# 1/rms spread over the partitions: from diagonal matrices to broadcast columns

## The chip, the core and the metric

The kernel runs on one core of a Trainium2 chip. The metric is the device time of one execution in microseconds (us). Before the change it is 2209.36 us, the median of three runs (2209.26 to 2209.65).

## The reference

One decoder layer over a sequence of 2048 tokens with 1024 features, all in float32. It normalizes x, projects it to the inputs of two groups of heads (a gated linear recurrence "HGRN" with four heads, and a sliding-window attention with eight heads), mixes their outputs back, and then runs a gated MLP of width 2816 with a short causal convolution. RMS norms stand at four places; three of them go over the 1024 features of a token, and one over the 128 values of an HGRN head.

```python
def rmsnorm(x, w, eps=EPS):
    xf = x.astype(jnp.float32)
    inv = lax.rsqrt(jnp.mean(xf * xf, axis=-1, keepdims=True) + eps)
    return (xf * inv * w.astype(jnp.float32)).astype(x.dtype)
...
    for l in range(DEPTH):
        u = rmsnorm(h, norm_mix_w[l])
        proj = u @ w_in[l]
...
        o_hg = rmsnorm(o_hg, hg_norm_w[l]).reshape(B, S, HG_VAL_WIDTH)
...
        h = h + mix @ w_out[l]
        v = rmsnorm(h, norm_ffn_w[l])
        gate = causal_depthwise_conv(v @ w_gate[l], conv_w[l], conv_b[l])
        h = h + (jax.nn.silu(gate) * (v @ w_up[l])) @ w_down[l]
    return rmsnorm(h, final_norm_w)
```

## The kernel before

The sequence is processed in two halves of 1024 tokens. Everything is held transposed: features on the 128 partitions, tokens along the free dimension. A matrix of float32 values is split into two float32r parts, high and low, and a product is made of three passes (high x high, low x high, high x low), so that the large products are streams of matmuls with 512 moving columns (`unit`, L190; `pair_unit`, L731; `product`, L915).

For each half the stages are: load and split of x, the projections and the heads (`hgrn` and `attend`, which are interleaved as generators), the output projection (`out_proj`), the gate and up projections (`gate_up`), and the down projection (`down`), which also loads the x of the next half or, in the second half, writes the output (`finish`). The gate, up and down products use a scheme with seven instead of eight block products, whose operands are sums formed on VectorE, and whose results accumulate in the banks X, Y and Z; ScalarE must copy X out between two of its products (L747).

The weight of a norm is folded into the operands; 1/rms of a token is applied to the results. It is a value per token, so it lies along the free dimension and has to be the same on all 128 partitions. This is the work of the class `Stats`:

- `add` squares one tile of features and adds it into `acc`, a tile of 128 partitions by the tokens.
- `inverse` sums `acc` over the partitions: for each 128 tokens, one matmul with that piece of `acc` as weights and one column of ones moving (L249). The sums come out with the tokens on the partitions, one column for each 128 tokens. `rsqrt` turns them into 1/rms with thirteen operations on VectorE (L158 to L168), an integer estimate and three Newton steps. Then one VectorE operation multiplies the unit matrix `ident` with these columns (L253), so that `acc` holds one diagonal matrix for each 128 tokens.
- `spread` multiplies a matrix of ones with these diagonal matrices, 512 columns at a time (L263): the sum over partitions of a diagonal matrix is its diagonal, now on every partition. ScalarE copies the result from its bank into `acc` (L266), or, where `bank` is given, the reader takes it from the bank.

There are nine such pairs of inverse and spread: over 1024 tokens for the first norm of each half ("x") and for the second ("h", during the first gate unit), over 512 tokens for three parts of the final norm ("o", "o2"), and over 256 tokens for the last two quarters. `rsqrt` is also called eight times in `hgrn` (L581). `ident` is made at the start by GpSimd (L84 to L87) and is also the moving operand of the transposes (L336, L408, L553, L592) and the mask of the diagonal blocks (L459).

The order of the instructions on each engine is set by a scheduler at build time: it simulates the program, and so a change at one place can change the order elsewhere. The pool `hp` with the tag "m" has eight slots, which tiles take in turn; the x tiles of the first load are its first users. 

Of the kernel before, what the change touches and what calls it, by code (L numbers as in the profile page):

```python
# [8 lines left out]
F32 = mybir.dt.float32  # L9
F32R = mybir.dt.float32r  # L10
U32 = mybir.dt.uint32
I32 = mybir.dt.int32
AF = mybir.ActivationFunctionType
ALU = mybir.AluOpType
# [3 lines left out]
P = 128  # L18
D = 1024
KT = D // P  # L20
# [10 lines left out]
EPS = 1e-6  # L31
# [18 lines left out]
def hymba_layer(ctx: ExitStack, tc: tile.TileContext, a: dict, out: bass.AP):  # L50
    nc = tc.nc

    def pool(name, bufs=1, space=None, stack=ctx, **kw):
        if space is not None:
            kw["space"] = space
        return stack.enter_context(tc.tile_pool(name=name, bufs=bufs, **kw))

    cp = pool("const")
    xp = pool("x")
    wp = pool("w")  # L60
    hp = pool("h")
    sp = pool("small", bufs=2)
# [6 lines left out]
    def ps(kind, name):  # L69
        return spaces[kind].tile([P, 512], F32, tag=kind, name=name)  # L70
# [3 lines left out]
    def halves():  # L74
# [5 lines left out]
    ones = cp.tile([P, P], F32, name="ones")  # L80
    nc.vector.memset(ones, 1.0)
    warm = cp.tile([P, 1], F32, name="warm")
    nc.scalar.activation(warm, ones[:, 0:1], AF.Sigmoid)
    ident = cp.tile([P, P], F32, name="ident")  # L84
    nc.gpsimd.memset(ident, 1.0)
    nc.gpsimd.affine_select(out=ident, in_=ident, compare_op=ALU.is_equal, fill=0.0,
                            base=0, pattern=[[-1, P]], channel_multiplier=1)  # L87

    idle = ps("at", "idle")
    for _ in range(WARM):  # L90
# [63 lines left out]

    def rsqrt(ss, n, scale, keep=None):

        ms = sp.tile([P, n], F32, tag=f"ms{n}", name="ms")
        nc.vector.tensor_scalar(ms, ss, scale, EPS, op0=ALU.mult, op1=ALU.add)  # L158
        y = sp.tile([P, n], F32, tag=f"y{n}{keep}", name="y")
        yi = y.bitcast(I32)  # L160
        nc.vector.tensor_scalar(yi, ms.bitcast(I32), 1, None, op0=ALU.logical_shift_right)
        nc.vector.tensor_scalar(yi, yi, -1.0, float(0x5F3759DF), op0=ALU.mult, op1=ALU.add)
        nc.vector.tensor_scalar(ms, ms, -0.5, None, op0=ALU.mult)
        t = sp.tile([P, n], F32, tag=f"t{n}", name="t")
        for _ in range(3):
            nc.vector.tensor_tensor(t, y, y, op=ALU.mult)
            nc.vector.tensor_tensor(t, t, ms, op=ALU.mult)
            nc.vector.scalar_tensor_tensor(y, t, 1.5, y, op0=ALU.add, op1=ALU.mult)  # L168
        return y
# [56 lines left out]
    class Stats:  # L226
# [16 lines left out]
        def inverse(self, keep):  # L243

            n = self.acc.shape[-1]
            nt = n // P
            st = ps("hg", "pst")
            for c in range(nt):
                nc.tensor.matmul(st[:, c:c + 1], self.acc[:, c * P:(c + 1) * P], ones[:, 0:1],  # L249
                                 start=True, stop=True)  # L250
            rs = self.rs = rsqrt(st[:, 0:nt], nt, 1.0 / D, keep)
            dg = self.acc
            return nc.vector.tensor_tensor(dg.rearrange("p (c t) -> p c t", t=P),  # L253
                                    ident.unsqueeze(1).to_broadcast([P, nt, P]),
                                    rs.unsqueeze(2).to_broadcast([P, nt, P]), op=ALU.mult)

        def spread(self, bank=None):

            n = self.acc.shape[-1]
            w = min(n, 512)  # L260
            for b in range(n // w):
                pb = ps(aux[b % 2 if bank is None else bank], "pinv")[:, 0:w]
                nc.tensor.matmul(pb, ones, self.acc[:, b * w:(b + 1) * w], start=True, stop=True)  # L263
                if bank is not None:
                    return pb
                nc.scalar.copy(self.acc[:, b * w:(b + 1) * w], pb)  # L266
# [166 lines left out]
    def hgrn(hf, h, X, invb, vs, WG, mix, p, fu=None):  # L433
# [140 lines left out]
        for c in range(TT):  # L574
# [4 lines left out]
            marks["po"] = nc.tensor.matmul(o, Q[:, cs], prev, start=False, stop=True)  # L579
            nc.scalar.activation(on[:, c], o, AF.Square, accum_out=ss[:, c:c + 1])  # L580
        rs = rsqrt(ss, TT, 1.0 / P)  # L581
        if h == HG - 1:
            mix[h] = new_x()
# [441 lines left out]
    for hf in range(NH):  # L1025
        X, kv, invb, rs, f0 = nxt
        with ExitStack() as st:
            p = pool(f"mix{hf}", stack=st, reuse_waits="tile")
# [36 lines left out]
        with ExitStack() as st:  # L1065
            p = pool(f"ffn{hf}", stack=st, reuse_waits="tile")
# [64 lines left out]
```

## Time and profile before

| | |
|---|---|
| median of 3 runs | 2209.36 us |
| the profiled execution, its time | 2211.5 us |
| the profiled execution, its span (first to last instruction) | 2209.8 us |
| mean granted clock of TensorE | 0.995 |
| instructions | 29508 |

In the lines of the profile, PE is TensorE (matmul), PEld its weight loads, DVE VectorE, ACT ScalarE, POOL GpSimd, SP SyncE. A line of the timeline gives the start in us, the duration in us, the engine, the line of the kernel, the operation, the tiles written and read, the shape, and how many instructions are merged; in brackets stands how long the engine was idle before, and what ended that. A duration of several merged instructions reaches from the first start to the last end. Matmuls are pipelined, so the step from one start to the next is what a matmul costs, not its duration. A line of the windows gives for a stretch the busy time of PE, PEld, DVE, ACT and POOL (with their instructions), the granted clock of TensorE, the busy share of the DMA engines, and GB/s.

### The profile page before, as it was taken

To read this page: it belongs to the slowest core of one execution; us is meant where nothing else is said; L and a number is where in the kernel's file an instruction comes from. 1 tells how busy PE (TensorE), PEld (TensorE's weight loads), DVE (VectorE), ACT (ScalarE), POOL (GpSimd) and SP (SyncE) were. 2 spreads that over 40 slices of the span, in tenths; PEclk is the share of its full clock that TensorE was granted. 3 is DMA by queue.
4 is the path that set the end of the run, shared out by engine and by line. 5 is a ranking of instruction groups with operands and counts; after the bars stand their busy time and mean duration, and the time that the engine had idled before them with its cause. 6 is when DMAs were issued, how large, how long until landed. Compare 5 with 4: busy or idle time off the path is not lost.

```text
span 2209.8 us, 29508 instructions
## 1 busy us (share of the span) xinstructions
PE 2182.2 (99%) x11406; PEld 1832.6 (83%) x11406; DVE 1643.8 (74%) x2488; ACT 1050.9 (48%) x1845; POOL 6.3 (0%) x27
## 2 busy tenths in 40 slices
PE   9999999999999999999999999999999999999998
PEld 7988988878888888888889889888788888888887
DVE  6568568688887888786856666577888888887766
ACT  6446554464444445335625455535544444444353
POOL 1000000000000000000000000000000000000000
PEclk9999999999999999999999999999999999999999
DMA  4101112323233234964631111204132323259643
GB/s 154 50 30 50 37 43 68 121 71 112 95 113 101 96 119 159 374 219 162 200 124 51 36 43 41 67 29 142 55 128 82 125 90 119 95 190 388 226 136 129
DMA packets 94214, 257.91 MB, mean 117 GB/s; under 512 B 11578, under 2 KB 17402, under 8 KB 94074
## 3 DMA queue, kind: packets, MB, share of 16 engines
q1 hardware_dynamic: 88128, 251.70, 33.6%
q10 hardware_dynamic: 5946, 4.34, 0.7%
q8 instruction: 89, 1.46, 0.3%
q14 instruction: 51, 0.42, 0.1%
HBM read 195.10 MB, written 57.15 MB: 114 GB/s over the span
## 4 chain that ended last, share of the span: by engine, by line
PE 94%; DVE 4%; ACT 1%; DMA 0%; issue 0%; SPq 0%; DVEq 0%; ACTq 0%
PE X L741 7%; PE X L743 7%; PE X L742 7%; PE pop L208 6%; PE hq L208 4%; PE q L208 4%; PE f L208 4%; PE g L208 4%; PE pdx L923 4%; PE pdx L924 4%; PE pdx L925 4%; PE Y L741 4%; PE Y L742 4%; PE Y L743 4%; PE pdy L924 3%; PE pdy L923 3%
## 5 line engine op out<-in xcount | busy, mean ns | idle before, releaser
L619 ACT CAST whi<-raw 128x1024 fp32r<-128x1024 f32 x88 | 92.7, 1053 | 104.3 <-PE X L742 64.5
L742 PE MATMUL X<-T,whi 128*128 128x512 f32 x352 | 136.9, 389 | 0.0
L743 PE MATMUL X<-T,wlo 128*128 128x512 f32 x352 | 136.9, 389 | 0.0
L741 PE MATMUL X<-T,whi 128*128 128x512 f32 x352 | 136.9, 389 | 0.0
L807 DVE SCALAR_TENSOR_TENSOR y<-ga,cw,y 128x1024 f32<-128x1024 f32 x88 | 112.5, 1278 | 30.9 <-ACT y L805 30.9
L747 ACT COPY u<-X 128x512 f32<-128x512 f32 x88 | 51.6, 586 | 130.0 <-PE X L743 129.6
L620 DVE TENSOR_TENSOR wlo<-raw,whi 128x1024 fp32r<-128x1024 f32 x88 | 107.1, 1217 | 0.0
L184 ACT CAST whi<-raw 128x1024 fp32r<-128x1024 f32 (+2 forms) x61 | 62.7, 1034 | 82.1 <-PE q L208 31.9
L620 DVE TENSOR_TENSOR xld<-raw,xhd 128x1024 fp32r<-128x1024 f32 x72 | 80.7, 1131 | 19.8 <-ACT xhd L619 19.5
L619 ACT CAST xhd<-raw 128x1024 fp32r<-128x1024 f32 x72 | 69.7, 978 | 43.8 <-DMA raw<-act0T 15.8
L208 PE MATMUL pop<-XL,whi 128*128 128x512 f32 x256 | 86.7, 396 | 2.1 <-DVE XL L220 2.1
L208 PE MATMUL pop<-XH,wlo 128*128 128x512 f32 x256 | 85.5, 392 | 0.7 <-DVE wlo L185 0.7
L208 PE MATMUL pop<-XH,whi 128*128 128x512 f32 x256 | 85.1, 398 | 0.2
L185 DVE TENSOR_TENSOR wlo<-raw,whi 128x1024 fp32r<-128x1024 f32 (+2 forms) x61 | 73.0, 1203 | 9.0 <-ACT whi L184 9.0
L741 PEld LDWEIGHTS X<-T,whi 128*128 128x128 f32 x352 | 66.1, 188 | 13.7
L742 PEld LDWEIGHTS X<-T,whi 128*128 128x128 f32 x352 | 66.1, 188 | 13.7
L743 PEld LDWEIGHTS X<-T,wlo 128*128 128x128 f32 x352 | 66.1, 188 | 13.7
L923 PE MATMUL pdx<-xhd,hid 128*128 128x512 f32 x192 | 74.3, 391 | 1.0 <-ACT hid L619 1.0
L924 PE MATMUL pdx<-xld,hid 128*128 128x512 f32 x192 | 74.8, 389 | 0.0
L741 PE MATMUL X<-T,Sh 128*128 128x512 f32 x176 | 69.0, 392 | 5.4 <-ACT s L747 5.4
L925 PE MATMUL pdx<-xhd,lod 128*128 128x512 f32 x192 | 73.7, 389 | 0.0
L611 PE MATMUL pvv<-whi,XH 128*128 128x256 f32 x256 | 73.5, 288 | 0.0
(362 smaller groups left out, 6564.9 us busy)
## 6 DMA issues: line engine op xcount, KB each, us to landing
wr<-in_w_down SPq DMA_DIRECT2D x90, 512.0 KB, 5.1
raw<-in_w_gate SPq DMA_DIRECT2D x44, 512.0 KB, 3.6
raw<-in_w_up SPq DMA_DIRECT2D x44, 512.0 KB, 3.5
raw<-act0T SPq DMA_DIRECT2D x20, 512.0 KB, 5.5
raw<-act1T SPq DMA_DIRECT2D x20, 512.0 KB, 10.1
act0B<-y SPq DMA_DIRECT2D x33, 256.0 KB, 2.5
act1B<-y SPq DMA_DIRECT2D x33, 256.0 KB, 2.3
raw<-in_w_out SPq DMA_DIRECT2D x16, 512.0 KB, 5.5
```

Of the source, the lines that this page charges most:

```text
L185: nc.vector.tensor_tensor(lo[:, c], raw[:, c], hi[:, c].bitcast(F32), op=ALU.subtract)
L208: nc.tensor.matmul(o[b], w, x[:, bs], start=f, stop=l)
L611: nc.tensor.matmul(o[:, 0:256], xh[:, t], hi[:, c], start=kt == 0, stop=False)
L619: nc.scalar.copy(h, src)
L620: (eng or nc.vector).tensor_tensor(l, src, h.bitcast(F32), op=ALU.subtract)
L741: nc.tensor.matmul(o, wh[:, ws], xh, start=i == 0 and not more, stop=False, skip_group_check=more)
L742: nc.tensor.matmul(o, wh[:, ws], xl, start=False, stop=False, skip_group_check=more)
L743: nc.tensor.matmul(o, wl[:, ws], xh, start=False, stop=i == 3, skip_group_check=more)
L807: nc.vector.scalar_tensor_tensor(y, g[:, w:w + HALF], C.cw[:, ft, w:w + 1], y, op0=ALU.mult, op1=ALU.add)
L923: nc.tensor.matmul(o, wh[:, i, c], ah[:, i, cols], start=f, stop=False, skip_group_check=more)
L924: nc.tensor.matmul(o, wh[:, i, c], al[:, i, cols], start=False, stop=False, skip_group_check=more)
L925: nc.tensor.matmul(o, wl[:, i, c], ah[:, i, cols], start=False, stop=l, skip_group_check=more)
```

## The change

The unit matrix is made in a slot of the pool `hp` and copied by ScalarE into a float32r tile, `identr`; `ident` becomes a float32 view of it. `rsqrt` computes -0.5 (mean + eps) at once and gets the integer estimate from it with one operation: eleven operations instead of thirteen. `inverse` no longer makes diagonal matrices; it splits 1/rms into two float32r parts, `rh` and `rl`, each of as many columns as there are groups of 128 tokens. `spread` takes one column of such a part, broadcast to 128 columns, as the weights, and the unit matrix as the moving operand: each output row is the transposed column. The two parts are added in the bank. This takes two matmuls for each 128 tokens, where one float32 matmul took 512.

```diff
@@ -81,10 +81,13 @@
-    ident = cp.tile([P, P], F32, name="ident")
-    nc.gpsimd.memset(ident, 1.0)
-    nc.gpsimd.affine_select(out=ident, in_=ident, compare_op=ALU.is_equal, fill=0.0,
+    unit_ = hp.tile([P, P], F32, tag="m", name="unit", bufs=KT)
+    nc.gpsimd.memset(unit_, 1.0)
+    nc.gpsimd.affine_select(out=unit_, in_=unit_, compare_op=ALU.is_equal, fill=0.0,
                             base=0, pattern=[[-1, P]], channel_multiplier=1)
+    identr = cp.tile([P, P], F32R, name="identr")
+    nc.scalar.copy(identr, unit_)
+    ident = identr.bitcast(F32)
...
@@ -154,13 +157,12 @@
         ms = sp.tile([P, n], F32, tag=f"ms{n}", name="ms")
-        nc.vector.tensor_scalar(ms, ss, scale, EPS, op0=ALU.mult, op1=ALU.add)
+        nc.vector.tensor_scalar(ms, ss, -0.5 * scale, -0.5 * EPS, op0=ALU.mult, op1=ALU.add)
         y = sp.tile([P, n], F32, tag=f"y{n}{keep}", name="y")
-        yi = y.bitcast(I32)
-        nc.vector.tensor_scalar(yi, ms.bitcast(I32), 1, None, op0=ALU.logical_shift_right)
-        nc.vector.tensor_scalar(yi, yi, -1.0, float(0x5F3759DF), op0=ALU.mult, op1=ALU.add)
-        nc.vector.tensor_scalar(ms, ms, -0.5, None, op0=ALU.mult)
+        nc.vector.tensor_scalar(y.bitcast(I32), ms.bitcast(I32), -0.5, float(0x5F3759DF - 2 ** 22 - 2 ** 30),
+                                op0=ALU.mult, op1=ALU.add)
...
@@ -249,10 +251,9 @@
             rs = self.rs = rsqrt(st[:, 0:nt], nt, 1.0 / D, keep)
-            dg = self.acc
-            return nc.vector.tensor_tensor(dg.rearrange("p (c t) -> p c t", t=P),
-                                    ident.unsqueeze(1).to_broadcast([P, nt, P]),
-                                    rs.unsqueeze(2).to_broadcast([P, nt, P]), op=ALU.mult)
+            self.parts = rh, rl = [sp.tile([P, nt], F32R, tag=f"{t}{nt}{keep}", name=t) for t in ("rh", "rl")]
+            nc.vector.tensor_copy(rh, rs)
+            nc.vector.tensor_tensor(rl, rs, rh.bitcast(F32), op=ALU.subtract)
 
         def spread(self, bank=None):
...
@@ -260,7 +261,12 @@
                 pb = ps(aux[b % 2 if bank is None else bank], "pinv")[:, 0:w]
-                nc.tensor.matmul(pb, ones, self.acc[:, b * w:(b + 1) * w], start=True, stop=True)
+
+                for c in range(w // P):
+                    for i, r in enumerate(self.parts):
+                        col = b * w // P + c
+                        nc.tensor.matmul(pb[:, c * P:(c + 1) * P], r[:, col:col + 1].to_broadcast([P, P]), identr,
+                                         start=i == 0, stop=i == 1)
                 if bank is not None:
                     return pb
                 nc.scalar.copy(self.acc[:, b * w:(b + 1) * w], pb)
```

## The prediction

> **What bounds the kernel now.** I read the page first (busy shares, then the chain that ended last), then the list of waits of TensorE, then the timeline around the places that the change touches. All durations come from the one profiled execution: its span is 2209.8 us, its own time 2211.5 us, so 1.7 us lie around the span; the three unprofiled runs have a median of 2209.36 us, 2.1 us under the profiled one. I make the sum against the span and carry the difference over to the median.
>
> ```profile
> PE 2182.2 (99%) x11406; PEld 1832.6 (83%) x11406; DVE 1643.8 (74%) x2488; ACT 1050.9 (48%) x1845; POOL 6.3 (0%) x27
> ...
> PE 94%; DVE 4%; ACT 1%; DMA 0%; issue 0%; SPq 0%; DVEq 0%; ACTq 0%
> ```
>
> TensorE is busy for 99% of the span and holds 94% of the chain. So an edit can change the time in three ways only: it changes how long TensorE's own stream of instructions is, it changes one of the few holes in that stream, or it changes the tail after the last large product. The holes are few; these are the two largest rows of the waits of TensorE (in total, times, longest):
>
> ```profile
> PE X L741 <- ACT s L747: 5.4, 2, 2.8
> PE pinv L263 <- DVE invb L253: 2.9, 1, 2.9
> ```
>
> Only the second belongs to the code that changes, and it occurs once, in the tail. Of the nine places where 1/rms is spread, the other eight are covered by other products that stand between inverse and spread.
>
> **The spread on TensorE.** Before, one spread of 1024 columns is two float32 products of 512 columns, which the hardware runs as four instructions:
>
> ```profile
> 1579.34 0.39 PE L743 MATMUL Y<-B,S 128*128 128x512 f32 x1
> 1579.57 1.88 PE L263 MATMUL pinv<-invb,ones 128*128 128x512 f32 x4
> 1580.88 0.80 PE L741 MATMUL Z<-B,whi 128*128 128x512 f32 x1
> 1581.52 0.40 PE L742 MATMUL Z<-B,whi 128*128 128x512 f32 x1
> ```
>
> From 1579.57 to 1581.52 there are 1.95 us; one normal step of 0.23 us (1579.34 to 1579.57) belongs to the Z product, so the spread takes 1.72 us of the stream, 0.86 us for 512 columns. The kernel spreads four times 1024 columns, three times 512 and twice 256. Leaving out the last 256, which are in the tail, that is 11 banks of 512, 9.46 us, and one of 256.
>
> After, each 128 columns take two instructions with 128 moving columns and a weight load of their own: 8 pairs for 512 columns, 88 pairs for the 11 banks, 4 for the 256. Their price is not in the trace: no weight there is a broadcast column. The nearest row is a stream of pairs in which the moving part is almost nothing (one column) and the 128x128 load sets the pace:
>
> ```profile
> 469.12 0.94 PE L249 MATMUL pst<-ones,invb 128*128 128x1 f32 x8
> 469.92 0.49 PE L741 MATMUL Y<-T,Sh 128*128 128x512 f32 x1
> 470.25 0.39 PE L742 MATMUL Y<-T,Sh 128*128 128x512 f32 x1
> ```
>
> Eight pairs run from 469.12 to 469.92, and the next product then takes 0.33 instead of 0.23 us: 0.90 us, 0.1125 us a pair. Those weights are float32. For float32r weights with few moving columns there is one place, the scores of the first block:
>
> ```profile
> 100.59 0.22 PE L372 MATMUL psc<-KS,qh 128*128 128x128 f32 x1
> 100.65 0.27 PE L372 MATMUL psc<-KS,ql 128*128 128x128 f32 x1
> 100.76 0.34 PE L372 MATMUL psc<-KS,qh 128*128 128x256 f32 x1
> 100.93 0.28 PE L372 MATMUL psc<-KS,ql 128*128 128x256 f32 x1
> 101.05 0.28 PE L372 MATMUL psc<-KS,qh 128*128 128x256 f32 x1
> ```
>
> Single steps are 0.06, 0.11, 0.17 and 0.12 us; four take 0.46 us, 0.115 us each. I take 0.1125, since both rows agree that the load sets the pace. Then 88 pairs are 9.90 us against 9.46: **+0.44 us**; the single 256 is 0.45 against 0.43 us (half a bank), **+0.02 us**. The bounds: at the shortest step, 0.06 us, 88 pairs are 5.3 us, a gain of 4.2; at the 0.23 us of a 512-column step, if a short moving part or a broadcast weight cost as much as a long one, they are 20.2 us, a loss of 10.8.
>
> The Trainium skill has a rule that lies between (TensorE: Matmul & The Clock Gate, section Back-to-back issue gap): a sustained stream of load and matmul pairs at 128 columns takes about 81 ns a pair. By it the 88 pairs would be an estimated 7.1 us, a gain of 2.3 us. The trace does not agree for float32 weights (0.1125 us), and the four float32r pairs averaged 0.115 us, so the sum does not use it.
>
> **The work on VectorE that goes away.** The product with the unit matrix is done nine times, and 17 calls of rsqrt lose two operations each:
>
> ```profile
> L253 DVE TENSOR_TENSOR invb<-ident,y x7: 426/1218/1226, 38.0 to 2201.8; 128x1024 f32<-128x1024 f32 x4, 128x256 f32<-128x256 f32 x2, 128x512 f32<-128x512 f32 x1
> L253 DVE TENSOR_TENSOR sums<-ident,y x2: 680/686/692, 1101.5 to 1115.9; 128x512 f32<-128x512 f32 x2
> ```
>
> That is four times 1.22, three times 0.69 and twice 0.43 us, 7.8 us, and 34 small ones of 0.16 us (in the tail's rows below), 5.4 us; 18 new ones (rh, rl) at the same 0.16 us give back 2.9 us. VectorE is left with some 10 us less. Outside the tail I cost this at nothing: TensorE runs other products meanwhile, and no large row of its waits names these lines. If that cover were gone somewhere, the product would be worth up to 1.2 us there; since it gets shorter, it can only help. In the heads of the HGRN group the shorter rsqrt lies behind the same cover.
>
> **The tail.** Here every operation is on the path:
>
> ```profile
> 2199.48 0.16 DVE L158 TENSOR_SCALAR ms<-pst 128x2 f32<-128x2 f32 x1 [0.76 <-PE pst L249]
> ...
> 2200.08 0.16 DVE L166 TENSOR_TENSOR t<-y 128x2 f32<-128x2 f32 x1
> ...
> 2201.65 0.16 DVE L168 SCALAR_TENSOR_TENSOR y<-t,y 128x2 f32<-128x2 f32 x1
> 2201.84 0.43 DVE L253 TENSOR_TENSOR invb<-ident,y 128x256 f32<-128x256 f32 x1
> 2202.32 1.22 PE L263 MATMUL pinv<-invb,ones 128*128 128x256 f32 x2 [2.88 <-DVE invb L253]
> 2203.58 2.73 DVE L1014 TENSOR_TENSOR h<-h,pinv 128x256 f32<-128x256 f32 x8 [1.31 <-PE pinv L263]
> ```
>
> Between L158 and L166 lie L161, L162 and L163; one operation takes their place. From 2199.48 to 2203.58 are 4.10 us. Dependent small operations follow one another every 0.196 us (2200.08 to 2201.65 are eight steps, 1.57 us). After, the nine Newton operations start at 0.40 instead of 0.60 us; the last starts at 1.97, rh at 2.16, rl at 2.36, and rl ends at 2.52, where L253 ended at 2.79 (2201.84 plus 0.43). TensorE starts 0.05 us behind that, as now: 0.27 us gained. Then TensorE: now 1.26 us from 2202.32 to 2203.58. The clock is at half there (rows below), and at half clock eight pairs of L249 take 1.56 us, 0.195 us a pair:
>
> ```profile
> 1563.48 1.70 PE L249 MATMUL pst<-ones,invb 128*128 128x1 f32 x8
> 1565.04 0.77 PE L741 MATMUL Y<-T,Sh 128*128 128x512 f32 x1
> ```
>
> The first pair (rh) runs before rl is there. Three follow: a load, two steps and the last one's own duration, which by that row is 0.34 us (1.70 less seven steps), and 0.04 us until VectorE reads, as now: 0.2 + 0.39 + 0.34 + 0.04, some 1.0 us, 0.26 us gained. So **-0.53 us** in the tail. The bounds: at full clock (steps of 0.1125) about -0.9, and with steps of twice 0.23 us, a 512-column step at half clock, about +0.25.
>
> **The start.** The unit matrix now passes through ScalarE into a float32r tile, and its float32 original takes one of eight slots that the loads of x rotate through. The copy is about 0.3 us, ahead of the first cast of weights:
>
> ```profile
> 2.78 0.30 ACT L184 CAST whi<-raw 128x128 fp32r<-128x128 f32 x1
> 5.21 0.72 ACT L222 ACTIVATE XH<-x,nmw 128x512 fp32r<-128x512 f32 x1 [2.12 <-DMA x<-in_xT]
> ```
>
> The next operation waits 2.12 us for x, so the copy is hidden: nothing; without that cover it would be 0.3 us. The slot is free again long before the eighth load of x needs it.
>
> **The sum**: +0.44 + 0.02 - 0.53 = -0.07 us. The span becomes 2209.7 us, the median **2209.3 us**: no change.
>
> **What the new order does.** The scheduler has put TensorE's stream in another order in the attention stage and in the whole gate and up loop. In that loop I compared, in the two programs, how many products stand between two uses of a bank that ScalarE must empty in between: X between T2 and T3 has at least 10 before and 12 after, X between B11 and T2 at least 9 in both; and between the last use of a low weight part and the first use of its successor in the same buffer in the steady loop at least 24 before and 37 after. One distance gets shorter, Y between T1 and B22 in the first pair, from 22 to 15 products (3.4 us at 0.23 us each); the nine of X, where the hole is, stay the shortest. So I cost the order at nothing. The two large holes (X L741, 2.8 us at most) keep the same order around them.
>
> **The rivals.**
> 1. *The hole before X and the clock.*
>
> ```profile
> 350.00:400.00 50.00, 47.90 (x357) 40.01 (x356) 38.51 (x84) 16.59 (x62) 0.00 (x0) 1.00 0.07 22
> ...
> 450.00:500.00 50.00, 46.89 (x210) 37.73 (x209) 43.79 (x71) 30.96 (x50) 0.00 (x0) 1.00 0.23 74
> 1400.00:1450.00 50.00, 48.60 (x273) 42.03 (x270) 34.64 (x60) 26.05 (x51) 0.00 (x0) 0.97 0.30 95
> 1450.00:1500.00 50.00, 47.89 (x349) 39.33 (x349) 34.70 (x77) 18.41 (x64) 0.00 (x0) 1.00 0.10 30
> 1557.90:1561.30 3.40, 1.24 (x5) 1.05 (x6) 3.40 (x5) 3.15 (x6) 0.00 (x0) 1.00 0.67 200
> 1561.40:1568.10 6.70, 6.70 (x21) 5.61 (x20) 5.92 (x10) 1.85 (x3) 0.00 (x0) 0.50 0.14 54
> 1568.20:1571.60 3.40, 3.40 (x20) 2.92 (x19) 1.93 (x7) 1.26 (x3) 0.00 (x0) 1.00 0.00 0
> 2199.60:2206.00 6.40, 1.22 (x2) 0.50 (x2) 4.71 (x22) 0.00 (x0) 0.00 (x0) 0.50 0.17 57
> ```
>
> Behind the hole of the second half (1557) the clock (third number from the end) is 0.50 for 6.7 us and 21 matmuls run, as many as in 3.4 us at full clock: 3.3 us lost. Behind the equal hole of the first half, in 450 to 500, it stays 1.00. A shift of some tenths can move one hole in or out: 2206.0 us if the loss goes (chance 0.10), 2212.6 us if the first half gets one too (0.10). The Trainium skill says (TensorE: Matmul & The Clock Gate, Part 1) that the activity window is free-running and 3413 ns long. Two equal holes with one loss agree with that. The rows don't tell which hole will be hit, so the forecast leaves the losses as they are.
> 2. *Pairs cheaper than that load*: at 0.06 us a pair the stream gains 4.2 us and the tail 0.5: 2204.7 us. For it the one step of 0.06; against it the mean of 0.115. Chance 0.09. The 81 ns of the Trainium skill's page, cited above, point to this side.
> 3. *Slower: a broadcast column is a slow weight, or float32r is slow with 128 columns.* Place: the 92 covered pairs. At 0.23 us each, 21.2 us, they cost 11.3 us more than the 9.46 and 0.43 of now, and the tail loses 0.25: 2220.9 us. It decides from 0.113 us a pair on, where the 92 pairs have used up the tail's 0.53. For it: no such weight is in the trace. Against it: a 128-column float32r step of 0.11. Chance 0.07.
> 4. *The new order opens holes in attention.* By the windows above, TensorE is idle for 2.1 us in 350 to 400, 1.4 in 1400 to 1450 and 2.1 in 1450 to 1500; if these 5.6 us doubled, 2214.9 us. Against it: the same dependencies, and VectorE has less to do. Chance 0.06.
> 5. The change as forecast: 0.58, in 2207.5 to 2211.5 us.
>
> A change within 0.2% (4.4 us: 2204.9 to 2213.8) cannot be told from none. Faster than that is most of rival 2: 0.08. Slower: rivals 3 and 4, less the mild part of 4: 0.12. The rest, 0.80, is the same. The range is 2205.3 to 2213.4: it holds both cases of the clock and stops short of rivals 2, 3 and 4.
>
> **What would show it.** Right: 16 pairs of a 1024 spread in about 1.8 us in the timeline, steps of 0.11; L253 gone; from the first small operation of the last rsqrt to the first h<-h,pinv about 3.6 us instead of 4.1; the two X holes still of 2.6 to 2.8 us; TensorE still at 99%. Wrong: pairs of 0.06 or 0.2 us, a new row of over 1 us in the waits of TensorE, or other stretches at half clock.

## The result and the profile after

The changed kernel takes 2228.72 us (median of 5 runs, 2228.16 to 2230.89), the kernel before 2209.36 us beside it (5 runs, 2208.94 to 2211.84). The ratio worked out from the runs is 1.0082 with a 95% interval of 1.0071 to 1.0094; the two medians alone give 1.0088. By the medians it is slower by 19.4 us, outside the predicted range of 2205.3 to 2213.4 us. The profiled execution of the changed kernel has a span of 2226.4 us, 16.6 us more than the one of before, at the same mean granted clock of 0.995.

The page of the changed kernel, busy times first, then the chain:

```profile
PE 2196.8 (99%) x11476; PEld 1838.6 (83%) x11476; DVE 1636.5 (74%) x2463; ACT 1049.9 (47%) x1844; POOL 6.4 (0%) x27
...
PE 92%; DVE 4%; ACT 1%; DMA 1%; issue 1%; ACTq 0%; DVEq 0%; SPq 0%
```

TensorE is still busy for 99%, and it is busy 14.6 us longer (2182.2 before), with only 70 instructions more. So most of the loss isn't waiting: TensorE works longer. The waits of TensorE (in total, times, longest):

```profile
PE X L747 <- ACT s L753: 5.2, 2, 2.8
PE pdx L929 <- ACT hid L625: 3.4, 2, 1.8
PE pinv L268 <- DVE rh L255: 2.4, 1, 2.4
PE plev L521 <- DVE K L529: 2.1, 2, 1.4
```

The row of the X holes and that of the tail are as foreseen. Two rows are new at the top: the start of the down projection (pdx) and a place in the attention (plev). Before, they stood further down the same list:

```profile
PE pdx L923 <- ACT hid L619: 1.0, 2, 0.5
...
PE plev L515 <- DVE K L523: 0.7, 1, 0.7
```

All rows of that list together are 20.4 us before and 22.7 us after, 2.3 us of the 16.6. The two terms that the prediction had worked out are as it said. A spread of 1024 columns in the timeline (start, duration):

```profile
42.98 0.22 PE L268 MATMUL pinv<-identr,rh 128*128 128x128 f32 x1
43.04 0.28 PE L268 MATMUL pinv<-identr,rl 128*128 128x128 f32 x1
43.15 0.28 PE L268 MATMUL pinv<-identr,rh 128*128 128x128 f32 x1
...
44.60 0.27 PE L268 MATMUL pinv<-identr,rl 128*128 128x128 f32 x1
44.72 0.68 PE L210 MATMUL f<-XH,wlo 128*128 128x512 f32 x2
```

Sixteen pairs take 1.74 us (42.98 to 44.72), with steps of 0.11. The product behind them then needs 0.28 instead of 0.23 us until the next one starts, so the spread takes 1.79 us of the stream, 0.112 us a pair, where the old one took 1.72 us. And the tail:

```profile
2216.72 0.16 DVE L162 TENSOR_SCALAR ms<-pst 128x2 f32<-128x2 f32 x1 [0.79 <-PE pst L251]
...
2218.88 0.17 DVE L255 CAST rh<-y 128x2 fp32r<-128x2 f32 x1
2219.08 0.16 DVE L256 TENSOR_TENSOR rl<-y,rh 128x2 fp32r<-128x2 f32 x1
2219.10 0.47 PE L268 MATMUL pinv<-identr,rh 128*128 128x128 f32 x1 [2.42 <-DVE rh L255]
...
2220.25 2.74 DVE L1020 TENSOR_TENSOR h<-h,pinv 128x256 f32<-128x256 f32 x8 [1.01 <-PE pinv L268]
```

From 2216.72 to 2220.25 are 3.53 us, 4.10 before.

**Where TensorE works longer.** Three windows in the middle of the gate and up loop, which the diff doesn't touch (the numbers behind "PE busy" count its matmuls), first before, then after:

```profile
500.00:550.00 50.00, 50.00 (x223) 41.40 (x222) 42.05 (x56) 20.58 (x31) 0.00 (x0) 1.00 0.32 105
600.00:650.00 50.00, 50.00 (x223) 41.40 (x222) 41.31 (x53) 24.53 (x35) 0.00 (x0) 1.00 0.26 90
700.00:750.00 50.00, 50.00 (x222) 41.41 (x221) 42.09 (x56) 21.26 (x31) 0.00 (x0) 1.00 0.39 127
```

```profile
500.00:550.00 50.00, 50.00 (x219) 40.86 (x218) 42.20 (x55) 20.08 (x30) 0.00 (x0) 1.00 0.31 103
600.00:650.00 50.00, 50.00 (x219) 40.85 (x218) 38.58 (x49) 22.70 (x33) 0.00 (x0) 1.00 0.25 88
700.00:750.00 50.00, 50.00 (x219) 40.84 (x218) 42.33 (x56) 21.11 (x30) 0.00 (x0) 1.00 0.38 127
```

TensorE is busy without a gap and at full clock in both, yet gets through 219 matmuls instead of 223 in 50 us. The same instruction has become slower. The groups by shape (instructions, busy us, mean ns of one) say which, before and after:

```profile
L742 PE MATMUL Z<-B,whi 128*128 128x512 f32 x176 | 68.7, 390 | 0.0
L743 PE MATMUL Z<-B,wlo 128*128 128x512 f32 x176 | 68.5, 389 | 0.0
L743 PE MATMUL Y<-B,S 128*128 128x512 f32 x176 | 68.5, 389 | 0.0
```

```profile
L748 PE MATMUL Z<-B,whi 128*128 128x512 f32 x176 | 69.7, 396 | 0.0
L749 PE MATMUL Z<-B,wlo 128*128 128x512 f32 x176 | 69.4, 394 | 0.0
L749 PE MATMUL Y<-B,S 128*128 128x512 f32 x176 | 68.7, 391 | 0.0
```

Z<-B takes 5 to 6 ns more, Y<-B,S two. These durations have modelled ends; in time from start to start, which is what counts, the difference is clearer. I took the mean over all such steps of the two traces (ns, 173 to 176 steps in each group, 352 for X<-T,whi), and beside it the SBUF address that the built program gives to the moving operand and to the weights, modulo 256 bytes. 1st and 2nd are the passes of L741 and L742 (L747 and L748 after); the others are the third pass, L743 (L749):

```
                 before: step  moving/weights     after: step  moving/weights
Z<-B,whi (2nd)   226.7         64 / 64            233.2        192 / 64
Z<-B,wlo         227.0         64 / 64            232.5        192 / 64
X<-B,wlo         226.7         64 / 64            232.2        192 / 64
Y<-T,Sh (2nd)    226.8         64 / 64            232.6        192 / 64
X<-T,whi (1st)   226.7         64 / 64            227.9        64 / 64
Y<-B,S (1st)     226.7         64 / 64            227.7        64 / 64
```

The small pool (`sp`) stands in SBUF ahead of the pools that are opened for each stage. The new tiles rh and rl are ten tags in it, with two buffers each and 32 bytes a partition for a buffer: 640 bytes. So every tile of the stage pools begins 640 bytes later, xh2d for example at 157376 instead of 156736. 640 is two and a half times 256: the operands in the stage pools (B11, B21 and T1 of the gate and up products, those of the down products and of the second half) go from 64 to 192 modulo 256, while the weights (whi at 106816) and the operands in the earlier pools stay at 64.

Over all steps of the two traces from one product of 512 columns to another (a step of over 300 ns, which holds a wait or half clock, is left out):

```
before   moving 64, next weights 64     7419 steps, mean 227.3 ns
         moving 64, next weights 96      168 steps, mean 238.0 ns
after    moving 64, next weights 64     5371 steps, mean 227.9 ns
         moving 192, next weights 64    1742 steps, mean 232.4 ns
         moving 64, next weights 192     264 steps, mean 232.6 ns
         moving 64 or 192, next 224      167 steps, mean 235.9 ns
         moving 192, next weights 192     60 steps, mean 230.8 ns
above 227 ns in all: before 3.9 us, after 17.6 us
```

13.7 of the 16.6 us of the span are here. With the 2.3 us of waits (which hold the gain in the tail) and the 0.4 us of the spreads (0.07 us for each 1024 of the 5632 columns outside the tail) that makes 16.4.

### The profile page after: what moved, and what is told of

Read it like the earlier page. It is cut to its first block, busy times and chain, and to the rows that moved or that the text cites. A ratio compares the mean times of both kernels' runs of the same rounds, so it can differ in the third digit from the quotient of the medians.

```text
span 2226.4 us, 29573 instructions
## 1 busy us (share of the span) xinstructions
PE 2196.8 (99%) x11476; PEld 1838.6 (83%) x11476; DVE 1636.5 (74%) x2463; ACT 1049.9 (47%) x1844; POOL 6.4 (0%) x27
## 4 chain that ended last, share of the span: by engine, by line
PE 92%; DVE 4%; ACT 1%; DMA 1%; issue 1%; ACTq 0%; DVEq 0%; SPq 0%
PE X L748 7%; PE X L747 7%; PE X L749 7%; PE pop L210 6%; PE hq L210 4%; PE q L210 4%; PE f L210 4%; PE g L210 4%; PE pdx L929 4%; PE pdx L930 4%; PE pdx L931 4%; PE Y L747 4%; PE Y L748 3%; PE Y L749 3%; PE pdy L930 3%; PE pdy L929 3%
## 5 line engine op out<-in xcount | busy, mean ns | idle before, releaser
L748 PE MATMUL X<-T,whi 128*128 128x512 f32 x352 | 137.4, 390 | 0.0
L749 PE MATMUL X<-T,wlo 128*128 128x512 f32 x352 | 137.3, 390 | 0.0
L747 PE MATMUL X<-T,whi 128*128 128x512 f32 x352 | 137.2, 390 | 0.0
L753 ACT COPY s<-X 128x512 f32<-128x512 f32 x44 | 25.8, 586 | 114.6 <-PE X L749 114.6
L747 PEld LDWEIGHTS X<-T,whi 128*128 128x128 f32 x352 | 66.1, 188 | 15.0
L748 PEld LDWEIGHTS X<-T,whi 128*128 128x128 f32 x352 | 66.1, 188 | 14.4
L749 PEld LDWEIGHTS X<-T,wlo 128*128 128x128 f32 x352 | 66.1, 188 | 14.1
L747 PE MATMUL X<-T,Sh 128*128 128x512 f32 x176 | 70.0, 398 | 5.2 <-ACT s L753 5.2
```

The source lines that it names most:

```text
L747: nc.tensor.matmul(o, wh[:, ws], xh, start=i == 0 and not more, stop=False, skip_group_check=more)
L748: nc.tensor.matmul(o, wh[:, ws], xl, start=False, stop=False, skip_group_check=more)
L749: nc.tensor.matmul(o, wl[:, ws], xh, start=False, stop=i == 3, skip_group_check=more)
L753: nc.scalar.copy(t, o)
```

## The experiments

Three theories stood after this. *Places*: the step depends on where the moving operand and the weights stand relative to each other, and the change moved them. *Order*: the new order of the instructions costs. *The pairs*: the new spread itself costs beyond its own time. In the runs on places not one instruction changes its order; only addresses do. In the table, "net" is the mean time of a kernel's runs times their mean granted clock, that is, what it would take without stretches at lower clock; the rest is the time lost to them. The clock of a run is given to 0.001 (2.2 us). By the scatter of the runs, the standard error of a net value of e1 to e12 is 0.3 to 0.5 us (1.0 for e4), that of a time lost to the clock 0.5 to 1.1 us (1.4 for e2 and 2.0 for e10, which have four runs each).

| kernel | median us | ratio to before, 95% | net us | lost to the clock us |
|---|---|---|---|---|
| before (the four groups of runs) | 2209.5 to 2210.0 | 1 | 2200.6 | 9.4 |
| after | 2228.72 | 1.0071 to 1.0094 | 2217.9 | 11.1 |
| e1 after, stage pools back in place | 2216.61 | 1.0017 to 1.0037 | 2204.1 | 11.9 |
| e2 before, stage pools moved by 128 | 2222.00 | 1.0045 to 1.0075 | 2213.6 | 9.4 |
| e3 before, everything moved by 128 | 2209.98 | 0.9992 to 1.0010 | 2200.1 | 9.7 |
| e4 before, stage pools moved by 64 | 2221.86 | 1.0041 to 1.0067 | 2209.6 | 12.2 |
| e5 before with the new rsqrt | 2212.48 | 1.0004 to 1.0021 | 2201.4 | 11.3 |
| e6 after with the old rsqrt, in place | 2208.15 | 0.9989 to 1.0009 | 2200.4 | 9.0 |
| e7 before, second ga in place | 2206.59 | 0.9976 to 0.9993 | 2198.5 | 8.6 |
| e8 after, all in place | 2213.14 | 1.0005 to 1.0024 | 2201.4 | 12.0 |
| e9 as e8, old rsqrt | 2206.45 | 0.9976 to 0.9993 | 2198.0 | 9.0 |
| e10 after, everything moved by 128 | 2228.96 | 1.0064 to 1.0107 | 2218.4 | 11.1 |
| e11 as e8, new rsqrt in inverse alone | 2210.30 | 0.9988 to 1.0005 | 2199.5 | 10.2 |
| e12 as e8, new rsqrt in hgrn alone | 2207.67 | 0.9984 to 1.0001 | 2199.2 | 8.8 |

**e1 and e2: move the stage pools alone.** The same line of 128 unused bytes in the small pool, put into the changed kernel (640 + 128 = 3 x 256, so the stage pools stand at 64 again) and into the kernel before (they stand at 192, as in the changed kernel):

```diff
+    sp.tile([P, 32], F32, tag="pad", name="pad", bufs=1)
```

> The changed kernel with 128 unused bytes per partition in the small pool, so that everything in the pools of the stages (operands B11, T1, B21 among them) lies 128 bytes higher; the instructions and their order are those of the changed kernel. Theory 'place': in the changed kernel the new tiles rh and rl moved these operands by 640 bytes, from 64 to 192 modulo 256, while the weights stayed at 64, and a step of a 512-column product with operands at unequal places takes some 232 ns instead of 227. With 128 more bytes they are at 64 again: the steps of X, Y and Z return to 227 ns and the time to 2208 to 2213 us. Rival 'order' (the new order of the gate and up loop runs slower) and rival 'pairs' (the broadcast weights are dear): the time stays at 2228 us.

> The kernel before with the same 128 unused bytes; instructions and order as before. Theory 'place': its operands in the stage pools move from 64 to 192 modulo 256, their 512-column steps go from 227 to some 232 ns, and the time rises by 12 to 16 us, to 2221 to 2226 us. Rivals 'order' and 'pairs': 2209 us, as before.

The changed kernel falls from 2228.72 to 2216.61 us, the kernel before rises from 2209.45 to 2222.00. One window of e1, then the same of e2:

```profile
500.00:550.00 50.00, 50.00 (x223) 41.40 (x222) 43.28 (x55) 21.01 (x32) 0.00 (x0) 1.00 0.30 101
```

```profile
500.00:550.00 50.00, 50.00 (x219) 40.77 (x218) 41.23 (x53) 21.04 (x31) 0.00 (x0) 1.00 0.31 100
```

223 matmuls where the places are those of before, 219 where they are those of after, whichever kernel it is. In steps: e1 has 227.3 ns at 64/64 and 4.2 us above 227 ns in all; e2 has 1736 steps of 232.6 ns and 17.3 us. So 12.1 us of the 19.4 come from the places alone, with no instruction added, removed or reordered. But e1 was expected at 2208 to 2213 us if places were all, and it misses that: the remaining 7 us of e1 against before are something else.

**e3, e4 and e10: which place counts.** In e3 and e10 the 128 bytes go into the first pool, so that everything behind it moves; in e4 the small pool grows by 64 bytes in the kernel before.

```diff
+    cp.tile([P, 32], F32, name="cpad")
```

```diff
+    sp.tile([P, 16], F32, tag="pad", name="pad", bufs=1)
```

> The kernel before with 128 unused bytes in the first pool, so that all tiles, weights and moving operands alike, move from 64 to 192 modulo 256. If the unequal places of the two operands cost the time: 2209 us. If the place 192 itself is slow: every 512-column step is slower, some 7900 by 5 ns, about 2249 us. Rivals 'order' and 'pairs': 2209 us.

> The kernel before with 64 unused bytes in the small pool: operands of the stage pools at 128 modulo 256, weights and other operands at 64. If any inequality modulo 256 costs: 2215 to 2230 us. If only the distance of 128 bytes costs: 2209 us.

> The changed kernel with 128 unused bytes in the first pool, so that every tile behind it moves by 128: the operands of the stage pools go from 192 to 64 bytes modulo 256 and the weights and the other operands from 64 to 192. Nothing else differs. Theory (the two places relative to each other count): they are still unequal, 2228 us (2224 to 2231), with the steps of the stage pools' operands at 231 to 233 ns. Rival (the operands' own place counts): those operands stand where before's stood, 2216 us, with steps of 227 ns.

The same window of e3, e4 and e10:

```profile
500.00:550.00 50.00, 50.00 (x223) 41.39 (x222) 42.06 (x53) 21.48 (x32) 0.00 (x0) 1.00 0.32 101
```

```profile
500.00:550.00 50.00, 50.00 (x219) 40.85 (x219) 41.95 (x53) 21.79 (x33) 0.00 (x0) 1.00 0.30 102
```

```profile
500.00:550.00 50.00, 50.00 (x219) 40.87 (x219) 42.19 (x55) 20.08 (x30) 0.00 (x0) 1.00 0.32 105
```

The mean durations of a group are no guide here: that of Z<-B,whi (2nd) is 395 ns in e3, nearer to the 396 of the changed kernel than to the 390 of before, though its steps are as short as before.

With moving operands and weights both at 192 (e3) the kernel takes 2209.98 us, as before, and its 7424 steps at 192/192 have a mean of 227.3 ns: 192 is as good a place as 64. With operands at 128 and weights at 64 (e4) 1740 steps have 230.8 ns, and the kernel takes 2221.86 us. In e10 the operands of the stage pools stand at 64, where they stood before, but the weights at 192: 1742 steps of 232.4 ns, 2228.96 us, as the changed kernel. So it is the place of the moving operand relative to the weights modulo 256 that counts, and not where either stands by itself. Whole multiples of 256 don't matter: in before, the steps at 64/64 whose places differ by 0, 256, 512 or 768 bytes modulo 1024 have means of 227.1 to 227.4 ns.

**e7: a displaced tile that was there before.** Of the 168 slow steps of before (238.0 ns), 156 come ahead of gad, low weight parts of the down projection in the buffers of the tile ga, and 12 ahead of Sl in the same place. That tile has 1026 columns, 4104 bytes, so the second of its two buffers begins at 96 modulo 256. Padding it puts this right:

```diff
-            ga = [p.tile([P, 2 + HALF], F32, tag="ga", name="ga", bufs=2) for _ in range(2)]
+            ga = [p.tile([P, 64 + HALF], F32, tag="ga", name="ga", bufs=2)[:, 0:2 + HALF] for _ in range(2)]
```

> The kernel before with the tile ga padded from 4104 to 4352 bytes, so that its second buffer and the weights gad in it lie at 64 modulo 256 like all others, instead of 96. Theory 'place': the 168 steps ahead of such a weight fall from 238 to 227 ns and those around them from 230: 2 to 3 us less, 2206.5 to 2207.5 us. Rival: weights in that buffer are slow for another reason: 2209.4 us.

The time is 2206.59 us against 2209.67, and the net time 2.1 us shorter. All steps now have a mean of 227.1 ns, 0.9 us above 227 in all where before had 3.9.

**e5 and e6: the two halves of the change.** e5 is the kernel before with the new rsqrt alone. e6 is e1 with the thirteen operations of the old rsqrt, so it has the new spread, with the stage pools in place.

```diff
-        nc.vector.tensor_scalar(ms, ss, scale, EPS, op0=ALU.mult, op1=ALU.add)
+        nc.vector.tensor_scalar(ms, ss, -0.5 * scale, -0.5 * EPS, op0=ALU.mult, op1=ALU.add)
...
-        yi = y.bitcast(I32)
-        nc.vector.tensor_scalar(yi, ms.bitcast(I32), 1, None, op0=ALU.logical_shift_right)
-        nc.vector.tensor_scalar(yi, yi, -1.0, float(0x5F3759DF), op0=ALU.mult, op1=ALU.add)
-        nc.vector.tensor_scalar(ms, ms, -0.5, None, op0=ALU.mult)
+        nc.vector.tensor_scalar(y.bitcast(I32), ms.bitcast(I32), -0.5, float(0x5F3759DF - 2 ** 22 - 2 ** 30),
+                                op0=ALU.mult, op1=ALU.add)
```

(e5; e6 is the changed kernel with these lines the other way round and the line of e1.)

> The kernel before with the rsqrt of eleven operations alone; all tiles stay where they were, and the order changes in a few places of the attention stage only. Theory: the tail gets 0.2 us shorter and nothing else happens, 2209.2 us. Rival: the six microseconds that the changed kernel keeps with its operands back in place (2216.6 against 2209.5 us) come with the rsqrt's new order: 2213 to 2216 us.

> The changed kernel with the old rsqrt and 128 unused bytes in the small pool, so that the operands of the stage pools are at 64 modulo 256. Theory: the spread by columns brings the new order, with the cast of the last short operand ahead of the cast of hid at the start of down, and the few microseconds that are left: 2214 to 2217 us, with over 1 us of waits of pdx on hid in each half. Rival (they come with the rsqrt): 2209 us.

e5 fits neither expectation well: it is 1.0013 times before, more than the theory's 2209.2 us and a little less than the rival's 2213 to 2216. For e6 I had expected the second part of the loss with the spread. It isn't there: e6 takes 2208.15 us, no different from before, and 8.5 us less than e1 (6.6 us by the means), from which it differs by the two operations of rsqrt and the order that the scheduler then makes. So the pairs, the third theory, cost nothing beyond their own time. The wait at the start of down is gone with them; the row of e1, then of e6:

```profile
PE pdx L930 <- ACT hid L626: 4.0, 2, 2.5
```

```profile
PE pdx L931 <- ACT hid L627: 1.0, 2, 0.5
```

How does a shorter rsqrt make a wait in the down projection? By the order that the scheduler makes of it. The start of down in the changed kernel, in the timeline:

```profile
897.49 0.39 PE L931 MATMUL pdx<-xhd,lod 128*128 128x512 f32 x1
...
897.90 0.62 ACT L625 CAST xhd<-raw 128x512 fp32r<-128x512 f32 x1 [1.14 <-DMA raw<-act0B]
...
898.42 1.04 ACT L625 CAST hid<-wr 128x1024 fp32r<-128x1024 f32 x1
...
899.51 0.50 PE L929 MATMUL pdx<-xhd,hid 128*128 128x512 f32 x1 [1.64 <-ACT hid L625]
```

and before:

```profile
888.87 1.05 ACT L619 CAST hid<-wr 128x1024 fp32r<-128x1024 f32 x1 [1.84 <-PE X L742]
...
889.07 0.39 PE L925 MATMUL pdx<-xhd,lod 128*128 128x512 f32 x1
...
889.97 0.50 PE L923 MATMUL pdx<-xhd,hid 128*128 128x512 f32 x1 [0.51 <-ACT hid L619]
```

Before, ScalarE goes straight to the weights hid. In the changed kernel a cast of a late operand (xhd, 512 columns) stands ahead of them in its queue and waits for a DMA, and hid, which TensorE needs first, waits behind it: TensorE idles for 1.64 and, in the second half, 1.76 us instead of 0.51 each. The fourteen traces agree: in the five with a wait of over 1 us here (after, e1, e8, e10, e11) the cast of 512 columns stands ahead of hid and has waited 0.9 to 1.9 us for its DMA, in both halves; in the nine others it doesn't, and the wait is 0.5 us. No run changes ScalarE's order alone.

e5 says that the new rsqrt alone doesn't make this wait (pdx 1.0, plev 0.7, as before); it costs 0.8 us net and 1.8 us of clock. Where these come from was not found.

**e8 and e9: everything in place, with the new rsqrt and with the old.** In e8 rh and rl take 256 bytes instead of 640, and ga is padded as in e7; e9 is e8 with the old rsqrt.

```diff
-            self.parts = rh, rl = [sp.tile([P, nt], F32R, tag=f"{t}{nt}{keep}", name=t) for t in ("rh", "rl")]
+            self.parts = rh, rl = [sp.tile([P, max(nt, 4)], F32R, tag=f"{t}{max(nt, 4)}", name=t)[:, 0:nt] for t in ("rh", "rl")]
```

> The changed kernel with the parts rh and rl in four shared slots (256 bytes instead of 640, so that the operands of the stage pools are at 64 modulo 256) and ga padded as well; the order is that of the changed kernel. Theory: as with 128 unused bytes, less the 2 to 3 us of gad: 2213 to 2215 us; the steps of all 512-column products at 227 ns. Rival 'order': 2226 us or more.

> The spread of the change with the thirteen-operation rsqrt of before; rh and rl in four shared slots of the small pool, and the ga tile padded so that both of its buffers stand at 64 bytes modulo 256, as all other operands do. Theory of places: the two gains add. The spread with its stage pools back in place ran at 2208.15 us and the padding took 2209.67 to 2206.59, so 2205.1 us (2203.5 to 2207), a 512-column step of 227 ns at every place, and no wait of TensorE pdx on ScalarE hid among the costly ones. Rival (the shorter stage comes with a chance of clock or of order, not with places): 2208 us, as the spread alone.

Both have steps of 227.1 ns everywhere. e8 takes 2213.14 us, e9 2206.45. The 6.7 us between them are again the two operations of rsqrt: 3.4 us net and 3.0 us of clock. The waits of TensorE in e8:

```profile
PE pdx L929 <- ACT hid L625: 3.3, 2, 2.1
...
PE plev L521 <- DVE K L529: 2.1, 2, 1.4
```

and of e9:

```profile
PE pdx L930 <- ACT hid L626: 1.0, 2, 0.5
...
PE plev L522 <- DVE K L530: 0.7, 1, 0.7
```

The two rows differ by 3.7 us, about the net difference. The traces also show where clock is lost. Three windows of e1, the first 2.1 us behind the long wait of plev (1.4 us, until 1464.4), the second 0.2 us behind that of pdx (2.5 us, until 1992.0), the third right after it:

```profile
1466.50:1469.90 3.40, 3.40 (x30) 2.88 (x30) 3.06 (x7) 0.00 (x0) 0.00 (x0) 0.51 0.00 0
1992.20:1995.60 3.40, 3.40 (x9) 2.65 (x9) 3.40 (x5) 1.24 (x2) 0.00 (x0) 0.50 0.95 314
1995.60:1999.00 3.40, 3.40 (x16) 2.76 (x16) 3.32 (x4) 1.61 (x2) 0.00 (x0) 1.00 1.00 354
```

A stretch of 3.4 us at half clock costs 1.7 us. The four kernels with the long wait of plev in the second half (after, e1, e8, e10) all have such a stretch about 1.5 to 2.4 us behind it, and none of the other ten has one between 1450 and 1550 us. Of the ten waits of pdx of over 1 us, the three longest (2.1 us in e8, 2.3 in e11, 2.5 in e1) are followed by one within 0.7 us, the seven of 1.2 to 2.0 us are not. Two stretches are 3.4 us, about what e1 and e8 lose to the clock beyond e6 and e9. That is one execution of each kernel, and no run makes a wait without the rest, so the cause is likely but not shown. Nor is it all: e5, with neither wait, loses 1.8 us more to the clock than before.

**e11 and e12: which of the calls of rsqrt.** e8 with the new rsqrt in `inverse` alone (e11) and in `hgrn` alone (e12), the old one at the other place.

```diff
-        rs = rsqrt(ss, TT, 1.0 / P)
+        rs = rsqrt13(ss, TT, 1.0 / P)
```

```diff
-            rs = self.rs = rsqrt(st[:, 0:nt], nt, 1.0 / D, keep)
+            rs = self.rs = rsqrt13(st[:, 0:nt], nt, 1.0 / D, keep)
```

> The changed kernel with four shared slots for rh and rl and the padded ga tile; the eleven-operation rsqrt is kept in the inverse alone, and hgrn has the thirteen operations of before. Theory (the rest of the loss, 2213.1 against about 2205, comes with hgrn's shorter rsqrt and the other order that it brings to the attention): 2205 us (2203.5 to 2207.5), and no wait of TensorE pdx on ScalarE hid above 1 us. Rival (it comes with the shorter rsqrt of the inverse): 2213 us, with that wait at 3 us.

> The other half of the run before: the changed kernel with four shared slots for rh and rl and the padded ga tile, the eleven-operation rsqrt in hgrn alone and the thirteen operations of before in the inverse. ScalarE's order around the casts of hid is then that of the spread alone. Theory (the two halves add: with both the kernel took 2213.14 us, with the inverse's alone 2210.30, with neither 2206.45): 2209.3 us (2207.5 to 2211), the wait of TensorE pdx on ScalarE hid back at 1.0 us, the wait of plev on VectorE K at 2.1 us as with both. Rival (hgrn's shorter rsqrt costs only together with the inverse's): 2206.5 us (2205 to 2207.5), and the wait of plev at 0.7 us.

I had put it down to hgrn, and that was wrong: e11 takes 2210.30 us and has the wait, e12 2207.67 and doesn't. Of e11, then of e12:

```profile
PE pdx L945 <- ACT hid L641: 3.8, 2, 2.3
...
PE plev L537 <- DVE K L545: 0.7, 1, 0.7
```

```profile
PE pdx L945 <- ACT hid L641: 1.0, 2, 0.5
...
PE plev L537 <- DVE K L545: 0.7, 1, 0.7
```

So e12's expectation failed too: its time lies within the expected range, but the wait of plev is that of the rival. The wait of pdx comes with the shorter rsqrt of the inverse, the longer wait of plev only with both (and, by e5, either only together with the new spread). The parts don't add up: 3.9 us for the inverse and 1.2 for hgrn, which is no more than the noise, against 6.7 for both together. That is what one expects if the cost belongs to an order and not to an operation.

## Why the prediction was wrong

**The step that failed is the price of what isn't edited.** The prediction named three ways in which the time can change, the first of them "how long TensorE's own stream of instructions is", and then counted only instructions that are added and removed. For all others it took "one normal step of 0.23 us" as given. That step has changed: 227 ns before, 231 to 236 for some 2200 of 7600 products after. In the sum the term is missing; it measures 13.4 us in the steps of the trace (after against e1), 12.1 us in the medians. The diff shows what causes it, though not as a cost: new tiles in a pool that stands ahead of others. The profile before showed that a step can differ, too: 168 of the steps that I took as equal had 238 ns.

**"So I cost the order at nothing" failed as well**, by some 3.5 us net, and 3 us of clock beside it (e1 against e6, e8 against e9). I compared distances in TensorE's order, in the gate and up loop; the new wait lies where the loop ends, in ScalarE's order. Rival 4 had the kind of mechanism right (new holes by a new order) but not the place: in the three windows of attention from which it took 5.6 us of idle time, TensorE idles for 5.3 us after. The waits of plev grew by 1.4 us there, but those of poT fell from 1.2 to 0.2, and pdx is not in attention. That its 2214.9 us stands near e8, which has this loss and not that of the places, is chance.

**The terms that were worked out were right.** The pairs were costed at 0.1125 us, with what the next product takes longer, and measure 1.79/16 = 0.112 in the same way (1.74/16 = 0.109 without). The tail was to fall from 4.10 to about 3.6 us and fell to 3.53. VectorE's work away from the tail was costed at nothing, and the start too; e6, which holds all of that but the shorter rsqrt, is at 2208.15 us against the forecast 2209.3 and can't be told from before. Rivals 2 and 3, cheaper or dearer pairs, are ruled out by the 0.11 us. The 81 ns of the Trainium skill (TensorE: Matmul & The Clock Gate, section Back-to-back issue gap) do not hold for these pairs.

**Rival 1**, the clock, happened to cancel in the two profiled executions (0.995 in both), though the stretches at half clock stand at other places: after has one behind each X hole and one behind plev, before had one of twice the length behind the second X hole and one at 1441.8. It is real all the same: over the runs of e1 and e8 the clock takes 3 us more than over those of e6 and e9.

**The list of what would show it wrong** held "a new row of over 1 us in the waits of TensorE" and "other stretches at half clock", and both came. It held nothing for a product that isn't part of the change taking longer; the first thing to look at, the number of matmuls in an equal window, wasn't on it.

## What to carry to other kernels

A new tile, however small, moves everything that is allocated behind it: before a change is priced by its instructions, print the addresses of the large operands of both kernels and see whether moving operands and weights still stand at the same place modulo 256. When a saturated engine gets slower without new waits, count the same instruction in equal windows before looking for a cause in the edit. And a shorter operation in a scheduled kernel is a new order: compare the queues of all engines at the borders of the stages, where a cast that waits for a DMA can get ahead of one that is needed at once.

## What the runs showed of the hardware

The step of a 512-column float32r product on TensorE depends on the SBUF addresses of its operands: 227 ns where the moving operand and the weights that are loaded meanwhile are equal modulo 256 bytes (at 64/64 in before, e7 and e9, at 192/192 in e3), 230.8 ns at 128/64, 232.4 to 232.6 ns at 192/64 and 64/192, 236 to 238 ns where the weights stand at 96 or 224 (231.7 at 64/160 in e4). The sixty steps at 192/192 among others in the changed kernel have 230.8 ns, and its steps at 64/64 in the gate and up loop 228 instead of 226.7; in before the steps right ahead of and behind the 168 slow ones have 231 and 229 ns, so the neighbours count too; why isn't known. The clock was granted in full (1.00) in the windows of the gate and up loop. The Trainium skill (SBUF — State Buffer, section Operand start alignment) says that an operand may start at any multiple of its element size, and that the runs behind this timed nothing; the runs here add the time: all these places are allowed, but they are not equally fast.

The best versions are e7, which is the kernel before with the padded ga, and e9, which has the new spread, the old rsqrt and all operands in place: 0.9984 of the kernel before each, with an interval of 0.9976 to 0.9993. The spread by broadcast columns adds nothing to the padding that these runs can tell.
